# More pairs of the SwiGLU by block products, and a third tile for the second half of a pair's raw weights

## The chip, the cores and the metric

The kernel runs on one core of one Trainium2 chip. The metric is the time of one execution on the device in microseconds (us). A profile of one execution, with the start and the duration of every instruction, goes with it. The engines are TensorE (PE; its weight loads are listed apart as PEld), VectorE (DVE), ScalarE (ACT), GpSimd (POOL) and SyncE (SP), whose queue issues nearly all DMAs.

## The reference

One decoder layer over 512 tokens of width 1024 in float32: a SwiGLU FFN, a pair of gated token mixers (short convolution and Mamba-2), cross-attention over 256 memory tokens, a second SwiGLU FFN, and a final norm. The change touches the two FFNs alone.

```
def swiglu(u, w_gate_up, w_down):
    gate, up = jnp.split(u @ w_gate_up, 2, axis=-1)
    return (jax.nn.silu(gate) * up) @ w_down

h = h + 0.5 * swiglu(rmsnorm(h, ffn1_norm), ffn1_w_gate_up, ffn1_w_down)
...  mixers, attention
h = h + 0.5 * swiglu(rmsnorm(h, ffn2_norm), ffn2_w_gate_up, ffn2_w_down)
out = rmsnorm(h, final_norm)
```

The inner width is 2816, which is 22 groups of 128 columns. The kernel keeps float32 accuracy by splitting each operand into a rounded part `hi` and a remainder `lo` (type fp32r), and by three matmuls for each product: hi x hi, hi x lo, lo x hi.

## The kernel before

Activations lie transposed: a tile is 128 features by 512 tokens, and `u` is eight such tiles with their `hi` and `lo`. Weights come from HBM as raw float32 tiles of 128 x 1024, 512 KB each; ScalarE casts them to `hi` (L105), VectorE subtracts to get `lo` (L106), and PE loads them as stationary 128 x 128 blocks.

An FFN runs over 22 *pairs*, a pair being 128 columns of gate and the same 128 of up. Pairs go in blocks of 6, 8 and 8 (0 to 5, 6 to 13, 14 to 21). Behind each block stands the *down projection* of what the block made: eight jobs, whose results are added to `h` (L371, L373).

A pair is computed in one of two ways, chosen by `seven(ct)`:

- *Plain* (`plain`): two raw tiles in the ring `wr` (three tiles), split, and 48 matmuls of 512 tokens into two PSUM tiles.
- *By block products* (`seven_a`, `seven_b`): up and gate, the two halves of the feature axis and the two halves of the tokens make a product of 2 x 2 matrices of blocks. It is formed from seven block products instead of eight, each of 12 matmuls of 256 tokens, 84 in all. The sums of weight blocks are made on VectorE and then split: `sa` (L297, L298), the raw tile `ca` of the ring `wr` reused in place (L301), and `sb` (L304). Sums of tokens (`th`, `tl`) are made once for each FFN, behind pair 1 (`token_sums`).

`seven_a(n)` holds the first half of a pair: 24 matmuls with the split of `sa` (`wh`, `wl`), then 24 with the split of `ca` (`xh`, `xl`); each 24 are followed by a ScalarE copy out of PSUM and a VectorE add into `ev` (L309 to L314). `seven_b(n)` holds the second half: 12 matmuls with the split of `sb`, 24 with the split of the second raw tile `db`, and then L325, L326, L330, L331 and `act` (Silu, L270, the split of the result into `sh` and `sl`). `seven_b(n)` is emitted behind `seven_a(n+1)`, or behind the plain pair that follows.

A pair by block products has two PSUM tiles, A and B, from a pool of five for all users (`PJ`); the second 24 matmuls of pair n are written into the bank that B of pair n-2 held, which L326 reads last.

Raw tiles by block products: `ca` comes from the ring `wr` (L293), `db` from a tag of its own with two tiles (L294). Both are issued on the SP queue, in order, and each load waits until the tile that it overwrites has been read for the last time. For `db` that is the split `xl<-db`.

The order of instructions on each engine is set when the program is built, by a scheduler in the framework: it takes instructions from further down the text where it expects an engine to be free, and on the chip every engine then runs its list in that order.

Of the kernel before, what the change touches and what calls it, by code (L numbers as in the profile page):

```python
# [20 lines left out]
F32 = mybir.dt.float32  # L21
# [5 lines left out]
P = 128  # L27
# [18 lines left out]

def seven(ct):

    return ct >= 4 and ct % 3 != 0


COL = {}
# [10 lines left out]
def layer(ctx: ExitStack, tc: tile.TileContext, a, out):  # L63
# [13 lines left out]
    def nm(s):  # L77
        uid[0] += 1
        return f"{s}_{uid[0]}"

    def ps(tag="pj"):
        return psp.tile([P, T], F32, tag=tag, name=nm(tag), bufs=PJ if tag == "pj" else 8 - PJ)
# [21 lines left out]
    def split(src, hi, lo):  # L104
        S.copy(out=hi, in_=src)  # L105
        V.tensor_tensor(out=lo, in0=src, in1=hi, op=ALU.subtract)  # L106

    def ring(tag, dt=F32R):
        return wp.tile([P, 1024], dt, tag=tag, name=nm(tag), bufs=3)
# [93 lines left out]
    def ffn(gname, wgu, wd, fin=None):  # L203
        fs = ExitStack()
        fp = fs.enter_context(tc.tile_pool(name=nm("fp"), bufs=1, reuse_waits="tile"))
# [11 lines left out]
        def split_pair(src):  # L217

            ws = [fp.tile([P, 1280], F32R, tag=t, name=nm(t), bufs=2) for t in ("xh", "xl")]
            split(src.rearrange("p (a n) -> p a n", a=2),  # L220
                  *(t[:, :2 * (512 + OFF)].rearrange("p (a n) -> p a n", a=2)[:, :, :512]
                    for t in ws))
            return ws

        def mm3(pt, w, off, xs, start, stop):

            hi, lo = w
            for k in range(4):
                c = slice(off + k * P, off + (k + 1) * P)
                xh, xl = xs[k]  # L230
                TE.matmul(pt, hi[:, c], xh, start=start and k == 0, stop=False,  # L231
                          skip_group_check=True)
                TE.matmul(pt, hi[:, c], xl, start=False, stop=False, skip_group_check=True)  # L233
                TE.matmul(pt, lo[:, c], xh, start=False, stop=stop and k == 3,  # L234
                          skip_group_check=True)

        def quad(k0, i):
            c = slice(i * H, (i + 1) * H)
            return [(u[k0 + k][0][:, c], u[k0 + k][1][:, c]) for k in range(4)]

        def tsum(i):
            c = slice(i * H, (i + 1) * H)
            return [(x[0][:, c], x[1][:, c]) for x in tq]
# [45 lines left out]

        def seven_a(ct):  # L290
            ca = ring("wr", F32)
            db = fp.tile([P, 1024], F32, tag="db", name=nm("db"), bufs=2)
            nc.sync.dma_start(out=ca, in_=wgu[ct][:, :1024])  # L293
            nc.sync.dma_start(out=db, in_=wgu[ct][:, 1024:])  # L294
            c, a_, d, b = ca[:, :512], ca[:, 512:], db[:, :512], db[:, 512:]
            s31 = fp.tile([P, 1024], F32, tag="sa", name=nm("sa"), bufs=2)
            V.tensor_tensor(out=s31[:, 512:], in0=c, in1=d, op=ALU.add)  # L297
            V.tensor_tensor(out=s31[:, :512], in0=c, in1=a_, op=ALU.add)  # L298
            w31 = ring("wh"), ring("wl")
            split(s31, *w31)  # L300
            V.tensor_tensor(out=c, in0=a_, in1=s31[:, 512:], op=ALU.add)  # L301
            w2a = split_pair(ca)
            s4 = fp.tile([P, 512], F32, tag="sb", name=nm("sb"), bufs=2)
            V.tensor_tensor(out=s4, in0=c, in1=b, op=ALU.add)  # L304
            A, B = ps(), ps()
            mm3(B[:, 0:H], w31, 512, tsum(0), True, True)
            mm3(B[:, H:], w31, 0, tsum(1), False, True)
            ev = fp.tile([P, T], F32, tag="ev", name=nm("ev"), bufs=2)
            S.copy(out=ev[:, 0:H], in_=B[:, 0:H])  # L309
            V.tensor_tensor(out=ev[:, 0:H], in0=B[:, H:], in1=ev[:, 0:H], op=ALU.add)  # L310
            mm3(A[:, 0:H], w2a, 512 + OFF, quad(0, 0), True, True)
            mm3(A[:, H:], w2a, 0, tsum(2), False, True)
            S.copy(out=ev[:, H:], in_=A[:, H:])
            V.tensor_tensor(out=ev[:, H:], in0=A[:, 0:H], in1=ev[:, H:], op=ALU.add)  # L314
            return ct, A, B, ev, s4, db
# [18 lines left out]
        for b1 in range(KF % SB, KF + 1, SB):  # L334
            b0 = max(0, b1 - SB)
            wait = None
            for ct in range(b0, b1):
                if seven(ct):
                    nxt = seven_a(ct)
                    if wait is not None:  # L340
                        seven_b(*wait)
                    wait = nxt
                else:
                    p = plain(ct)
                    if ct == 0:
                        r = rms(h, D, wk)
                    plain_out(ct, *p)
                    if wait is not None:
                        seven_b(*wait)
                        wait = None  # L350
                if ct == 1:
                    token_sums()
# [50 lines left out]
    with tc.tile_pool(name="mx", bufs=1, reuse_waits="tile") as mx:  # L403
# [183 lines left out]
        for g in range(NG):  # L587
            bt, ct, xs = nxt
# [350 lines left out]
```

## Time and profile before

| | |
|---|---|
| median of 3 runs | 1577.1 us (1576.55 to 1578.83) |
| the profiled execution | 1577.46 us |
| its span, first to last instruction | 1575.7 us |
| PE busy | 1553.4 us (99%) |
| VectorE busy | 1035.4 us (66%) |
| ScalarE busy | 735.7 us (47%) |
| mean busy share of the DMA queues | q1, the SP queue's: 32.0% |

The profile page lists busy time by engine, the chain of work that ended last, and groups of instructions by source line with their count, mean duration and the idle time ahead of them. The timeline lists single instructions with start and duration in us; idle time ahead of one, and what ended it, stands in brackets. Tile names have their buffer numbers left out there. The first FFN runs from 6.4 us to 357.1, the second from 1213.7 to the end.

### The profile page before, as it was taken

How to read it: one execution, taken by the hardware profiler on the slowest of the kernel's cores; microseconds unless marked ns; L12 is line 12 of the kernel's file. 1: busy time of each engine (PE TensorE's matmuls, PEld its weight loads, DVE VectorE, ACT ScalarE, POOL GpSimd, SP SyncE). 2: the span in 40 equal slices, each digit the busy share in tenths (PEclk: the TensorE clock that was granted, in tenths of full speed). 3: DMA queues.
4: the chain of work that ended last, by engine and by line, in shares of the span. 5: the costliest groups of instructions: out<-in, count | busy, mean ns of one | idle time of the engine just before them, and what ended most of it. 6: DMA issues, size and time to landing. Idle time of an engine off the chain costs nothing.

```text
span 1575.7 us, 20708 instructions
## 1 busy us (share of the span) xinstructions
PE 1553.4 (99%) x8259; PEld 1315.2 (83%) x8259; DVE 1035.4 (66%) x1503; ACT 735.7 (47%) x1091; POOL 10.4 (1%) x22
## 2 busy tenths in 40 slices
PE   8999999999999999999999999999999999999998
PEld 6989989987878787787888888888888888988986
DVE  7767667667694777847564544665556867767754
ACT  8424324446787583935332222444344633433533
POOL 0000000011000000000000000000000000000000
PEclk9999999999999999999999999999999999999999
DMA  5333333235343424333243222235204233332321
GB/s 204 108 114 98 104 107 107 70 121 181 102 121 107 134 75 139 103 100 99 87 137 104 94 94 97 97 114 187 80 27 134 78 111 109 106 94 94 108 80 54
DMA packets 54065, 168.70 MB, mean 107 GB/s; under 512 B 6337, under 2 KB 6849, under 8 KB 53969
## 3 DMA queue, kind: packets, MB, share of 16 engines
q1 hardware_dynamic: 51952, 160.77, 32.0%
q0 software_dynamic: 1584, 5.31, 0.9%
q8 instruction: 64, 1.05, 0.3%
q10 hardware_dynamic: 432, 1.31, 0.2%
q14 instruction: 33, 0.26, 0.1%
HBM read 163.10 MB, written 4.26 MB: 106 GB/s over the span
## 4 chain that ended last, share of the span: by engine, by line
PE 94%; DVE 2%; DMA 2%; ACT 1%; issue 1%; ACTq 0%
PE pj L134 19%; PE pj L133 19%; PE pj L132 19%; PE pj L231 10%; PE pj L233 9%; PE pj L234 9%; DMA ea<-acd 1%; PE ss L557 1%; PE ss L508 1%; PE ss L562 1%; PE pj L692 0%; PE pj L691 0%; PE pj L693 0%; PE ss L496 0%; PE ss L160 0%
## 5 line engine op out<-in xcount | busy, mean ns | idle before, releaser
L105 ACT CAST wh<-wr 128x1024 fp32r<-128x1024 f32 (+2 forms) x251 | 243.8, 972 | 513.6 <-PE pj L133 370.3
L106 DVE TENSOR_TENSOR wl<-wr,wh 128x1024 fp32r<-128x1024 f32 (+2 forms) x251 | 281.6, 1125 | 93.5 <-ACT wh L105 93.3
L134 PE MATMUL pj<-uh,wl 128*128 128x512 f32 (+1 forms) x712 | 278.8, 393 | 3.5 <-DVE wl L106 3.5
L132 PE MATMUL pj<-uh,wh 128*128 128x512 f32 (+1 forms) x712 | 280.3, 394 | 0.0
L133 PE MATMUL pj<-ul,wh 128*128 128x512 f32 (+1 forms) x712 | 279.3, 392 | 0.0
L134 PEld LDWEIGHTS pj<-uh,wl 128*128 128x128 f32 (+1 forms) x712 | 133.5, 188 | 32.2 <-DVE wl L106 3.7
L231 PE MATMUL pj<-uh,wh 128*128 128x512 f32 (+1 forms) x416 | 152.9, 368 | 6.4 <-ACT uh L141 6.4
L132 PEld LDWEIGHTS pj<-uh,wh 128*128 128x128 f32 (+1 forms) x712 | 133.4, 187 | 28.2 <-issue 0.5
L133 PEld LDWEIGHTS pj<-ul,wh 128*128 128x128 f32 (+1 forms) x712 | 133.5, 188 | 28.0 <-issue 0.3
L233 PE MATMUL pj<-ul,wh 128*128 128x512 f32 (+1 forms) x416 | 152.6, 367 | 0.0
L234 PE MATMUL pj<-uh,wl 128*128 128x512 f32 (+1 forms) x416 | 151.9, 366 | 0.0
L133 PE MATMUL pj<-sl,wh 128*128 128x512 f32 x344 | 134.4, 391 | 0.2
L132 PE MATMUL pj<-sh,wh 128*128 128x512 f32 x344 | 134.1, 391 | 0.0
L134 PE MATMUL pj<-sh,wl 128*128 128x512 f32 x344 | 134.0, 389 | 0.0
L231 PEld LDWEIGHTS pj<-uh,wh 128*128 128x128 f32 x416 | 78.5, 189 | 20.1 <-ACT uh L141 6.6
L233 PEld LDWEIGHTS pj<-ul,wh 128*128 128x128 f32 x416 | 78.9, 190 | 13.2 <-DVE ul L142 0.7
L234 PEld LDWEIGHTS pj<-uh,wl 128*128 128x128 f32 x416 | 78.5, 189 | 12.5
L371 DVE SCALAR_TENSOR_TENSOR dn<-pj,r 128x512 f32<-128x512 f32 x47 | 32.5, 691 | 75.8 <-PE pj L134 75.7
L133 PEld LDWEIGHTS pj<-sl,wh 128*128 128x128 f32 x344 | 64.6, 188 | 14.8 <-DVE sl L106 1.9
L134 PEld LDWEIGHTS pj<-sh,wl 128*128 128x128 f32 x344 | 64.6, 188 | 13.3
L132 PEld LDWEIGHTS pj<-sh,wh 128*128 128x128 f32 x344 | 64.5, 188 | 13.3 <-ACT sh L105 0.2
L400 DVE SCALAR_TENSOR_TENSOR cv<-cx,prm,cv 128x510 f32<-128x510 f32 (+2 forms) x72 | 52.3, 744 | 5.4 <-ACT cv L397 5.2
(280 smaller groups left out, 3044.3 us busy)
## 6 DMA issues: line engine op xcount, KB each, us to landing
wr<-in_w_in SPq DMA_DIRECT2D x80, 512.0 KB, 3.2
wr<-in_w_gu SPq DMA_DIRECT2D x62, 512.0 KB, 3.8
wr<-in_w_d SPq DMA_DIRECT2D x32, 512.0 KB, 3.6
db<-in_w_gu SPq DMA_DIRECT2D x24, 512.0 KB, 3.9
m<-acd SPq DMA_DIRECT2D x32, 256.0 KB, 3.7
wr<-in_w_os SPq DMA_DIRECT2D x32, 256.0 KB, 3.1
wr<-in_w_d SPq DMA_DIRECT2D x16, 384.0 KB, 3.3
ea<-acd SPq DMA_DIRECT2D x32, 128.0 KB, 4.7
```

Of the source, the lines that this page charges most:

```text
L105: S.copy(out=hi, in_=src)
L106: V.tensor_tensor(out=lo, in0=src, in1=hi, op=ALU.subtract)
L132: TE.matmul(pt, hi[:, s_], xh, start=(k == 0), stop=False)
L133: TE.matmul(pt, hi[:, s_], xl, start=False, stop=False)
L134: TE.matmul(pt, lo[:, s_], xh, start=False, stop=(k == nk - 1))
L231: TE.matmul(pt, hi[:, c], xh, start=start and k == 0, stop=False, skip_group_check=True)
L233: TE.matmul(pt, hi[:, c], xl, start=False, stop=False, skip_group_check=True)
L234: TE.matmul(pt, lo[:, c], xh, start=False, stop=stop and k == 3, skip_group_check=True)
L371: V.scalar_tensor_tensor(out=dn, in0=pd, scalar=0.5, in1=r, op0=ALU.mult, op1=ALU.mult)
L400: V.scalar_tensor_tensor(out=acc[:, d:], in0=x[:, :T - d], scalar=pc(wname, j0 + j), in1=acc[:, d:], op0=ALU.mult, op1=ALU.add)
L508: TE.matmul(pst, btok[:, cs], xe, start=True, stop=True)
L557: TE.matmul(yd[64 * hh:64 * hh + 64, cs], xdt[c][:, q0:q0 + 64], ms[hh][:, cs], start=True, stop=True)
```

## The change

`seven(ct)` is true for every pair from the fourth on (ct >= 3) instead of for two of three from the fifth on, and the tag `db` has three tiles instead of two.

```
 def seven(ct):
-    return ct >= 4 and ct % 3 != 0
+    return ct >= 3
...
         def seven_a(ct):
             ca = ring("wr", F32)
-            db = fp.tile([P, 1024], F32, tag="db", name=nm("db"), bufs=2)
+            db = fp.tile([P, 1024], F32, tag="db", name=nm("db"), bufs=3)
             nc.sync.dma_start(out=ca, in_=wgu[ct][:, :1024])
             nc.sync.dma_start(out=db, in_=wgu[ct][:, 1024:])
```

In each FFN 19 pairs go by block products instead of 12: the pairs 3, 6, 9, 12, 15, 18 and 21 are new. Pair 3 stands in the block of six, the others in the blocks of eight, which now hold no plain pair at all.

Since the framework orders the instructions anew, three places are shown as they stand in the two programs (line, operation, out<-in, with the number of each tile).

VectorE in the first block of eight, from the split of one `db` tile to the L297 that reads the load which goes next into the same tag. Before (`db_1143` is pair 8, `db_1471` pair 11; pair 9 between them is plain):

```order
L106 TENSOR_TENSOR xl_1346<-db_1143,xh_1345 128x2x512
L326 TENSOR_TENSOR xx_1259<-pj_1088,ev_1113 128x512
L106 TENSOR_TENSOR wl_1342<-sb_1158,wh_1341 128x512
L330 TENSOR_TENSOR gt_1262<-pj_1087,r_245 128x256
L331 TENSOR_TENSOR gt_1262<-xx_1259,r_245 128x256
L304 TENSOR_TENSOR sb_1413<-wr_1397,db_1398 128x512
L106 TENSOR_TENSOR xl_1410<-wr_1397,xh_1409 128x2x512
L270 SCALAR_TENSOR_TENSOR gt_1262<-xx_1259,gt_1262 128x512
L297 TENSOR_TENSOR sa_1474<-wr_1470,db_1471 128x512
```

After (`db_1261` is pair 8, `db_1648` pair 11, which takes its tile; this row of nine comes again, with other numbers, in each pair of the block):

```order
L106 TENSOR_TENSOR xl_1467<-db_1261,xh_1466 128x2x512
L270 SCALAR_TENSOR_TENSOR gt_1380<-xx_1377,gt_1380 128x512
L301 TENSOR_TENSOR wr_1518<-wr_1518,sa_1522 128x512
L325 TENSOR_TENSOR xx_1506<-ev_1304 128x256
L304 TENSOR_TENSOR sb_1534<-wr_1518,db_1519 128x512
L106 TENSOR_TENSOR sl_1386<-gt_1380,sh_1385 128x512
L310 TENSOR_TENSOR ev_1433<-pj_1408,ev_1433 128x256
L106 TENSOR_TENSOR wl_1592<-sb_1405,wh_1591 128x512
L297 TENSOR_TENSOR sa_1651<-wr_1647,db_1648 128x512
```

Between the two rows stand seven instructions in both, of 512 columns or fewer after the change.

VectorE in the first block of the first FFN, at the end of the token sums (`tq`, `tl`). Before; `wl_411` is the second half of pair 2's weights, `wl_451` and `wl_481` are pair 3's, and `sa_521` belongs to pair 4:

```order
L255 SCALAR_TENSOR_TENSOR tq_368<-tq_368,ug_365 128x256
L106 TENSOR_TENSOR wl_411<-wr_409,wh_410 128x1024
L106 TENSOR_TENSOR sl_322<-gt_317,sh_321 128x512
L106 TENSOR_TENSOR tl_361<-tq_355,th_360 128x1024
L257 SCALAR_TENSOR_TENSOR tq_368<-tq_368,ug_365 128x256
L106 TENSOR_TENSOR wl_451<-wr_449,wh_450 128x1024
L106 TENSOR_TENSOR wl_481<-wr_479,wh_480 128x1024
L106 TENSOR_TENSOR tl_374<-tq_368,th_373 128x1024
L297 TENSOR_TENSOR sa_521<-wr_517,db_518 128x512
```

After; `sa_451` belongs to pair 3, `sa_524` to pair 4, and `wl_455` is the split of the first:

```order
L255 SCALAR_TENSOR_TENSOR tq_368<-tq_368,ug_365 128x256
L106 TENSOR_TENSOR sl_322<-gt_317,sh_321 128x512
L257 SCALAR_TENSOR_TENSOR tq_368<-tq_368,ug_365 128x256
L106 TENSOR_TENSOR tl_361<-tq_355,th_360 128x1024
L106 TENSOR_TENSOR wl_411<-wr_409,wh_410 128x1024
L106 TENSOR_TENSOR tl_374<-tq_368,th_373 128x1024
L297 TENSOR_TENSOR sa_451<-wr_447,db_448 128x512
L298 TENSOR_TENSOR sa_451<-wr_447 128x512
L297 TENSOR_TENSOR sa_524<-wr_520,db_521 128x512
L301 TENSOR_TENSOR wr_447<-wr_447,sa_451 128x512
L106 TENSOR_TENSOR wl_455<-sa_451,wh_454 128x1024
```

Pair 3's two plain splits are gone, pair 2's second split stands behind `sl_322`, L257 and `tl_361`, and the block products begin one pair earlier.

PE at the same place, the second half of pair 2 (`pj_377` and `pj_378` are its two PSUM tiles), as the difference of the two programs:

```order
 L231 MATMUL pj_377<-uh_138,wh_410 128x512
 L233 MATMUL pj_377<-ul_139,wh_410 128x512
+L231 MATMUL pj_378<-uh_138,wh_410 128x512
+L233 MATMUL pj_378<-ul_139,wh_410 128x512
 L234 MATMUL pj_377<-uh_138,wl_411 128x512
 L231 MATMUL pj_377<-uh_142,wh_410 128x512
```

Two matmuls that need only `wh_410` have moved ahead of the first one that needs `wl_411`.

More of the change, by code (lines that the diff above doesn't have):

```diff
@@ L47, in seven @@
 def seven(ct):
-    return ct >= 4 and ct % 3 != 0
+    return ct >= 3
 COL = {}
@@ L291, in seven_a @@
             ca = ring("wr", F32)
-            db = fp.tile([P, 1024], F32, tag="db", name=nm("db"), bufs=2)
+            db = fp.tile([P, 1024], F32, tag="db", name=nm("db"), bufs=3)
             nc.sync.dma_start(out=ca, in_=wgu[ct][:, :1024])
```

## The prediction

> **What bounds the kernel now.** I read the page's busy shares first, then the chain of waits, then windows over the FFN stages, then VectorE's timeline there.
>
> ```profile
> PE 1553.4 (99%) x8259; PEld 1315.2 (83%) x8259; DVE 1035.4 (66%) x1503; ACT 735.7 (47%) x1091; POOL 10.4 (1%) x22
> PE 94%; DVE 2%; DMA 2%; ACT 1%; issue 1%; ACTq 0%
> ```
>
> TensorE (PE) is 94% of the chain that ends last. The share alone proves little, since matmul ends are modelled; so here are four windows by stage (length, then busy time and instruction count of PE, its weight loads, VectorE (DVE) and ScalarE (ACT)): one plain pair (the third), two consecutive pairs by block products, and the two last blocks of eight pairs, one in each FFN.
>
> ```profile
> core 0: us, PE busy (x) PEld busy (x) DVE busy (x) ACT busy (x) POOL busy (x), PEclk, DMA share, GB/s
> 32.10:42.98 10.88, 10.88 (x49) 9.01 (x48) 10.88 (x18) 7.52 (x10) 0.00 (x0) 1.00 0.26 79
> 53.86:73.41 19.55, 19.55 (x170) 19.55 (x169) 14.15 (x23) 9.24 (x15) 0.00 (x0) 1.00 0.38 115
> 231.70:313.10 81.40, 81.40 (x565) 75.73 (x564) 56.58 (x83) 34.92 (x49) 0.00 (x0) 1.00 0.27 84
> 1436.40:1517.80 81.40, 81.40 (x565) 75.73 (x564) 56.68 (x83) 34.91 (x49) 0.00 (x0) 1.00 0.27 81
> ```
>
> The clock is 1.00 throughout. A plain pair takes 10.88 us for 48 matmuls, 227 ns each from start to start. Two block-product pairs take 19.55 us for 168 matmuls, so 9.78 us a pair and 116 ns each. A block of eight with five block-product pairs should then be 5 x 9.78 + 3 x 10.88 = 81.5 us: it is 81.40. So in these stages PE is fed without a gap, and VectorE, busy 56.6 us of the 81.4, waits for it.
>
> **The change part by part.** *PE.* Seven pairs in each FFN (3, 6, 9, 12, 15, 18, 21) go from 48 wide matmuls to 84 half as wide: 10.88 - 9.78 = 1.10 us saved each, 14 x 1.10 = **-15.5 us** as long as PE is fed.
>
> *VectorE.* What feeds PE grows. Its timeline inside a block gives the interval from one start to the next, where nothing is waited for:
>
> ```profile
> 133.93 0.68 DVE L106 TENSOR_TENSOR wl<-sb,wh 128x512 fp32r<-128x512 f32 x1
> 134.53 0.42 DVE L330 TENSOR_TENSOR gt<-pj,r 128x256 f32<-128x256 f32 x1
> 134.86 0.41 DVE L331 TENSOR_TENSOR gt<-xx,r 128x256 f32<-128x256 f32 x1
> 135.19 0.68 DVE L304 TENSOR_TENSOR sb<-wr,db 128x512 f32<-128x512 f32 x1
> 135.79 1.22 DVE L106 TENSOR_TENSOR xl<-wr,xh 128x1024 fp32r<-128x1024 f32 x1
> 136.93 0.68 DVE L270 SCALAR_TENSOR_TENSOR gt<-xx,gt 128x512 f32<-128x512 f32 x1
> ```
>
> So 0.60 us for 512 columns, 0.33 for 256, 1.14 for 1024 (less than the durations, which overlap). A plain pair costs VectorE two splits of 1024 and three passes of 512, 4.1 us. A block-product pair costs 16 instructions: three of 1024 (3.42), eight of 512 (L297, L298, L301, L304, the sb split, L326, L270, the sl split: 4.80) and five of 256 (L310, L314, L325, L330, L331: 1.67), together 9.9 us. Before, eight pairs are 5 x 9.9 + 3 x 4.1 = 61.8 us under 81.4 of PE. After, they are 79.2 us under 8 x 9.78 = 78.2 us: the cover is gone, and every wait of VectorE inside a block counts. ScalarE stays covered: four casts, Silu, the sh cast and two copies are under 6 us a pair.
>
> *Waits of VectorE.* L297 needs the `db` load, which may start only when the split of the old `db` has read it (the last row is of all 24 such loads):
>
> ```profile
> 124.08 1.23 DVE L106 TENSOR_TENSOR xl<-db,xh 128x1024 fp32r<-128x1024 f32 x1 [0.67 <-ACT xh L105]
> 130.04 0.69 DVE L297 TENSOR_TENSOR sa<-wr,db 128x512 f32<-128x512 f32 x1 [1.65 <-DMA db<-in_w_gu]
> 154.66 1.22 DVE L106 TENSOR_TENSOR xl<-db,xh 128x1024 fp32r<-128x1024 f32 x1
> 155.90 0.33 SPq L294 DMA_DIRECT2D db<-in_w_gu  x1
> 159.58 0.69 DVE L297 TENSOR_TENSOR sa<-wr,db 128x512 f32<-128x512 f32 x1 [0.82 <-DMA db<-in_w_gu]
> DMA to landing us min/median/max: 3.7/3.9/6.6
> ```
>
> The issue follows the end of the split by 0.02 us. From the split's start to L297 it took 4.92 us in one case and 5.96 in the other, where a `wr` load was in flight; with the median landing it is 1.22 + 0.02 + 3.9 = 5.14. With three tiles the split of pair n frees the tile for pair n+3, and the new order has seven instructions between that split and L297 of n+3: 1.14 + 5 x 0.60 + 2 x 0.33 = 4.8 us. So the third tile is just not enough: L297 waits 0.1 to 1.2 us in each period; I take 0.3, near the median and the 4.92 case, as the `wr` load is issued some 3.5 us before. The period of VectorE is then 9.9 + 0.3 = 10.2 us against 9.78: it loses 0.4 us a pair.
>
> The Trainium skill, page "DMA: Bandwidth & Descriptors", section "Anatomy of one DMA", gives a fit of 2.0 us plus bytes at 436 GB/s, made on the GpSimd path: an estimate of 3.2 us for these 512 KB. By it the wait vanishes and the sum below is about -12.6; this trace has 3.7 at the least, and I go by the trace.
>
> *Who waits for VectorE.* On PE the first to stall is the second group of a first half (the `xh`/`xl` of `ca`), which takes the PSUM bank that L326 of the pair two back has to read. Worked through by hand from the last down matmul as zero, with these intervals and ScalarE's cast:
>
> ```profile
> L105 ACT CAST xh<-db 128x1024 fp32r<-128x1024 f32 x24 | 25.2, 1050 | 27.5 <-issue 15.5 <-PE pj L233 12.1
> ```
>
> pair 6's `xl<-db` runs at 6.8 (PE done with the old `xh` at 5.6, cast 1.05), so pair 9's `db` lands at 11.9 while VectorE is ready at 10.1; L326 of pair 7 ends at 27.3, and PE asks for the bank at 27.8. From there VectorE loses 0.4 a pair: PE asks at 37.6, 47.4, 57.1 and gets at 37.5, 47.7, 57.0 (pair 13's half has no later L298 beside it). PE's lag is 0.4 us a block, and five waits stand in it, so each 0.1 us more in a wait adds 0.5. Bounds: 0 (VectorE keeps up) and 0.4 + 5 x 0.85 = 4.7 (every landing like the 5.96 case). I take **0.9** a block of eight, four blocks: **+3.6 us**. Behind the block the 8 down jobs take 43 us of PE and let VectorE catch up.
>
> *The first block of each FFN.* Pair 3 now needs the token sums 10.88 us earlier:
>
> ```profile
> 36.16 1.22 DVE L106 TENSOR_TENSOR wl<-wr,wh 128x1024 fp32r<-128x1024 f32 x1
> 37.54 0.39 PE L231 MATMUL pj<-uh,wh 128*128 128x512 f32 x1
> 39.37 2.36 DVE L106 TENSOR_TENSOR wl<-wr,wh 128x1024 fp32r<-128x1024 f32 x2
> 41.64 1.22 DVE L106 TENSOR_TENSOR tl<-tq,th 128x1024 fp32r<-128x1024 f32 x1
> 42.98 0.39 PE L231 MATMUL pj<-uh,wh 128*128 128x512 f32 x1
> 1245.96 1.22 DVE L106 TENSOR_TENSOR tl<-tq,th 128x1024 fp32r<-128x1024 f32 x1
> 1247.75 0.39 PE L231 MATMUL pj<-uh,wh 128*128 128x512 f32 x1
> ```
>
> Pair 3's two splits (39.37) go, but pair 2's second split (36.16) moves behind `sl`, the last L257 and a `tl`: from 36.2, 0.60 + 0.33, 0.1 for a cast, 1.14 + 1.14, it ends at 39.5. PE starts that half at 37.54 and, with the two matmuls moved ahead, needs it at 38.45: 1.0 us lost. Then the last `tl`, L297, L298, L297, L301 and the split of the sums end at 44.3, against PE at 44.0 and its third matmul at 44.2: 0.1. Behind it PE's group for pair 4 has a matmul on pair 4's `xh` ahead, which ScalarE casts late: 0.5. That is 1.6 us; in the second FFN, where the last `tl` starts 1.79 us ahead of pair 3 instead of 1.34 (1245.96 and 1247.75, 41.64 and 42.98), it is 1.2. Bounds 0 and 5; I take **+2.9** for both.
>
> *Sum:* -15.5 + 3.6 + 2.9 = -9.0 us. The profiled execution took 1577.46 us (span 1575.7, 1.8 around it), so 1568.5; the median of the runs is 0.4 lower: **1568**. Loads of weights into PE, the mixer and the attention keep their instructions.
>
> **The rivals.** *Full gain:* VectorE never late, as the 56.6 us of 81.4 suggest for a mean over a block; against it the 79.2 over 78.2. 1577.1 - 15.5 = 1561.6.
>
> *VectorE becomes the bound and the change is slower:* place L297 in every period of the blocks of eight, price 0.85 us a wait as in the 130.04 row: lag 4.7 a block, 18.8 in four, so -15.5 + 18.8 + 2.9 = +6.2, 1583. It decides once a wait costs 0.55 us more than I take in the base of 0.4, where the lag reaches (15.5 - 2.9)/4 = 3.1. For it: one of the two cases shown. Against: that case had two loads in flight, and the new order sets them 3.5 us apart.
>
> *Weight loads set PE's pace:* 84 loads a pair instead of 48. If a load's 188 ns were a matmul's interval, a pair would be 15.8 us and the kernel 14 x 4.9 slower, 1646:
>
> ```profile
> L231 PEld LDWEIGHTS pj<-th,wh 128*128 128x128 f32 x192 | 36.0, 188 | 0.2
> ```
>
> Against it the 116 ns of the second window, loads included; break-even is 48/84 of 227, 130 ns. The Trainium skill, "TensorE: Matmul & The Clock Gate", section "Back-to-back issue gap", gives sustained spacings of 81 ns at 128 columns and 131 at 512, by which 84 narrow matmuls (over 6.8 us) lose to 48 wide ones (6.3 us); by that rule this change is slower, and the trace's 116 and 227 disagree.
>
> **How the numbers follow.** Forecast (lag 0 to 2.5 a block): 65%, own range 1562.5 to 1574. Full gain: 15%. VectorE-bound: 13%, weight loads: 1%. Between forecast and slower lies a rest of 6% near no change. A measurement of this kernel tells about 0.2% (3.2 us) from no change. So faster 0.80, same 0.06, slower 0.14. The range 1561 to 1579 leaves out the worst of the VectorE-bound case and a little below the full gain.
>
> **What would show it.** Right: windows over the new blocks of eight of 78.2 to 80.5 us; VectorE busy there with about 79 us of starts, idle mostly at L297 on `db`, five times a block by some tenths; PE idle only ahead of a matmul with `xh` of `ca`, released by L326, and at pair 2's second split and pair 4's first group. Wrong: a block over 81.4 us, PE waiting at every period (VectorE-bound); blocks at 78.2 with no PE gap (full gain); spacing of the narrow matmuls over 118 ns; or ScalarE named as the releaser in the blocks, which I hold to be covered.

## The result and the profile after

The changed kernel took 1565.27 us (median of 4 runs, 1564.51 to 1566.80) against 1577.41 us for the kernel before beside it: a ratio of 0.9919, 95% interval 0.9906 to 0.9931, or -12.1 us. The forecast was 1568 us, 1561 to 1579, and "faster" with 0.80. The profiled execution took 1564.51 us, its span 1562.7. One of the twelve executions with the third tile alone took 2223.16 us at a granted clock of 0.655 and is left out of its median below.

The busy shares and the chain of waits on the page of the kernel after:

```profile
PE 1539.7 (99%) x8763; PEld 1327.3 (85%) x8763; DVE 1109.1 (71%) x1657; ACT 763.1 (49%) x1147; POOL 10.4 (1%) x22
PE 88%; DVE 5%; DMA 3%; ACT 2%; issue 1%; ACTq 0%
PE pj L134 20%; PE pj L132 20%; PE pj L133 20%; PE pj L231 7%; PE pj L234 7%; PE pj L233 7%; DMA db<-in_w_gu 2%; DVE xl L106 1%; PE ss L557 1%; DVE wl L106 1%; PE ss L508 1%; PE ss L562 1%; DMA ea<-acd 0%; PE pj L692 0%; PE pj L691 0%
```

VectorE (DVE) is 74 us busier, TensorE (PE) 14 us less, and the chain that ends last now leaves TensorE for 12% of the span instead of 6%: through the `db` load and the splits. The chain alone would suggest that much is lost there. The windows by stage say otherwise. The kernel after, first its two first blocks of six pairs, then its four blocks of eight (columns: length; busy time and count of each engine; granted clock; DMA share; GB/s):

```profile
core 0: us, PE busy (x) PEld busy (x) DVE busy (x) ACT busy (x) POOL busy (x), PEclk, DMA share, GB/s
6.60:74.50 67.90, 66.86 (x409) 59.38 (x410) 63.22 (x101) 47.16 (x69) 0.00 (x0) 1.00 0.49 164
1207.20:1271.80 64.60, 64.01 (x410) 57.64 (x409) 53.70 (x85) 38.18 (x53) 0.00 (x0) 1.00 0.36 112
```

```profile
107.50:185.90 78.40, 78.27 (x674) 78.09 (x673) 73.03 (x117) 40.87 (x61) 0.00 (x0) 1.00 0.36 115
229.40:307.80 78.40, 78.25 (x674) 78.06 (x673) 70.66 (x112) 41.12 (x61) 0.00 (x0) 1.00 0.28 88
1304.80:1383.30 78.50, 78.35 (x673) 78.12 (x672) 73.00 (x117) 40.80 (x61) 0.00 (x0) 1.00 0.36 115
1426.90:1505.30 78.40, 78.40 (x674) 78.10 (x673) 70.54 (x112) 40.95 (x61) 0.00 (x0) 1.00 0.28 88
```

The same two first blocks in the kernel before:

```profile
6.40:73.40 67.00, 67.00 (x372) 58.24 (x373) 57.82 (x89) 45.22 (x65) 0.00 (x0) 1.00 0.47 159
1213.70:1278.20 64.50, 64.50 (x374) 56.86 (x373) 48.48 (x74) 36.16 (x49) 0.00 (x0) 1.00 0.33 104
```

The second and fourth block of eight went from 81.4 us to 78.4. The difference of the spans, 13.0 us, is made up so: the blocks of eight with the down jobs behind them -3.4, -3.5, -3.2 and (without its down jobs) -3.0; the two first blocks with theirs +0.9 and +0.2; the start +0.2; the middle (mixers, attention; the same instructions) -0.7; the end -0.5. Some 0.3 us of the +0.9 have nothing to do with the change: the first matmuls of an execution are slow for a time that differs from execution to execution (last section). From its 41st matmul on, the first block of the first FFN takes 55.4 us before and 55.9 after.

**Where TensorE still waits.** In the first block of each FFN, at pair 2's second split and at pair 4's first group (timeline of the kernel after, VectorE's row first; beyond the spacing the gaps are 1.06 us at 40.07 and 0.61 at 1237.38, for pair 2, and 0.31 each at 51.13 and 1248.43, for pair 4, which are not shown):

```profile
38.79 1.22 DVE L106 TENSOR_TENSOR wl<-wr,wh 128x1024 fp32r<-128x1024 f32 x1
...
40.07 0.50 PE L234 MATMUL pj<-uh,wl 128*128 128x512 f32 x1 [0.90 <-DVE wl L106]
...
1237.38 0.50 PE L234 MATMUL pj<-uh,wl 128*128 128x512 f32 x1 [0.45 <-DVE wl L106]
```

In the blocks of eight, once or twice a block, ahead of the group on `xh` of `ca`. VectorE and then TensorE in the block that begins at 107.5:

```profile
150.46 0.69 DVE L297 TENSOR_TENSOR sa<-wr,db 128x512 f32<-128x512 f32 x1 [0.19 <-DMA db<-in_w_gu]
...
152.00 1.22 DVE L106 TENSOR_TENSOR xl<-wr,xh 128x1024 fp32r<-128x1024 f32 x1
153.14 1.22 DVE L106 TENSOR_TENSOR wl<-sa,wh 128x1024 fp32r<-128x1024 f32 x1
154.27 0.68 DVE L326 TENSOR_TENSOR xx<-pj,ev 128x512 f32<-128x512 f32 x1
```

```profile
154.70 0.28 PE L234 MATMUL pj<-th,wl 128*128 128x256 f32 x1
155.10 0.36 PE L231 MATMUL pj<-uh,xh 128*128 128x256 f32 x1
```

L326 ends at 154.95, and TensorE's matmul, due at 154.82, starts at 155.10. The profile's page lists 0.7 us of idle time ahead of these matmuls in the whole execution, and puts 0.2 of it down to VectorE's L326:

```profile
L231 PE MATMUL pj<-uh,xh 128*128 128x256 f32 x304 | 85.9, 282 | 0.7 <-DVE xx L326 0.2
```

**VectorE's own waits** in that block (waits view, in all, times, longest):

```profile
DVE sa L297 <- DMA db<-in_w_gu: 2.8, 3, 1.8
```

### The profile page after: what moved, and what is told of

The parts are those of the page before. It is cut to its first block, busy times and chain, and to the rows that moved or that the text cites. A ratio compares the mean times of both kernels' runs of the same rounds, so it can differ in the third digit from the quotient of the medians.

```text
span 1562.7 us, 21928 instructions
## 1 busy us (share of the span) xinstructions
PE 1539.7 (99%) x8763; PEld 1327.3 (85%) x8763; DVE 1109.1 (71%) x1657; ACT 763.1 (49%) x1147; POOL 10.4 (1%) x22
## 4 chain that ended last, share of the span: by engine, by line
PE 88%; DVE 5%; DMA 3%; ACT 2%; issue 1%; ACTq 0%
PE pj L134 20%; PE pj L132 20%; PE pj L133 20%; PE pj L231 7%; PE pj L234 7%; PE pj L233 7%; DMA db<-in_w_gu 2%; DVE xl L106 1%; PE ss L557 1%; DVE wl L106 1%; PE ss L508 1%; PE ss L562 1%; DMA ea<-acd 0%; PE pj L692 0%; PE pj L691 0%
## 5 line engine op out<-in xcount | busy, mean ns | idle before, releaser
L105 ACT CAST wh<-wr 128x1024 fp32r<-128x1024 f32 (+3 forms) x223 | 214.4, 963 | 448.5 <-PE pj L133 341.8
L106 DVE TENSOR_TENSOR wl<-wr,wh 128x1024 fp32r<-128x1024 f32 (+3 forms) x223 | 247.5, 1112 | 70.2 <-ACT wh L105 70.0
L134 PE MATMUL pj<-uh,wl 128*128 128x512 f32 (+1 forms) x712 | 279.3, 394 | 3.5 <-DVE wl L106 3.5
L132 PE MATMUL pj<-uh,wh 128*128 128x512 f32 (+1 forms) x712 | 280.7, 394 | 0.0
L133 PE MATMUL pj<-ul,wh 128*128 128x512 f32 (+1 forms) x712 | 279.6, 393 | 0.0
L231 PE MATMUL pj<-uh,xh 128*128 128x256 f32 x304 | 85.9, 282 | 0.7 <-DVE xx L326 0.2
L234 PE MATMUL pj<-uh,xl 128*128 128x256 f32 x304 | 85.4, 281 | 0.0
L233 PE MATMUL pj<-ul,xh 128*128 128x256 f32 x304 | 85.4, 281 | 0.0
L231 PE MATMUL pj<-th,xh 128*128 128x256 f32 x304 | 84.7, 279 | 0.0
L231 PE MATMUL pj<-th,wh 128*128 128x256 f32 x304 | 84.5, 278 | 0.0
```

Source lines behind the costliest of these rows:

```text
L132: TE.matmul(pt, hi[:, s_], xh, start=(k == 0), stop=False)
L133: TE.matmul(pt, hi[:, s_], xl, start=False, stop=False)
L134: TE.matmul(pt, lo[:, s_], xh, start=False, stop=(k == nk - 1))
```

## The experiments

Two theories stood against each other from the start. One, the prediction's: in the blocks of eight VectorE has no room left, so its period sets the pace, and each wait at L297 counts. The other: TensorE is the bound as before, and VectorE has room that the count over the block does not show.

### The third tile alone, and the pairs alone

The third tile alone is the kernel before with

```
-            db = fp.tile([P, 1024], F32, tag="db", name=nm("db"), bufs=2)
+            db = fp.tile([P, 1024], F32, tag="db", name=nm("db"), bufs=3)
```

> The third db tile alone; the pairs by block products are those of the kernel before (4, 5, 7, 8, ...). Theory (TensorE is the bound there and VectorE, 61.8 of 81.4 us busy in a block of eight, waits for it): no change, 1577 within 1 us, blocks of eight still 81.4 us. Rival (waits for the db load already cost time before): faster by some us.

Measured: 1576.77 us, ratio 0.9992 (0.9983 to 1.0001); the block at 232.6 takes 81.5 us. By itself the third tile is worth nothing.

The pairs alone, the kernel after with

```
-            db = fp.tile([P, 1024], F32, tag="db", name=nm("db"), bufs=3)
+            db = fp.tile([P, 1024], F32, tag="db", name=nm("db"), bufs=2)
```

> All pairs from the fourth on by block products, but two db tiles as before. Theory (VectorE is the bound in the blocks, and each of its waits counts): with two tiles the split of pair n frees the tile for pair n+2, and the order has some 2 us of work between that split and L297 of n+2, against about 5 us from the split's start to the landing; so L297 waits some 2.4 us a period (1.7 to 3), VectorE's period is about 12.4 us against 9.78 of TensorE, a block of eight takes 88 to 91 us, and the kernel 1600 to 1615. Rival (VectorE has room, the third tile is not needed): blocks of 78 to 79 us, 1565 to 1568.

Measured: 1642.85 us, ratio 1.0416 (1.0389 to 1.0442): 66 us slower than before, 78 slower than with the third tile. The sign is the first theory's, the size is past its band. Its four blocks take 98.3 to 100.1 us. The waits view of the first of them, VectorE's row and then TensorE's, and windows over a few us of it (TensorE's busy time, then the granted clock, DMA share, GB/s):

```profile
DVE sa L297 <- DMA db<-in_w_gu: 8.6, 4, 2.6
```

```profile
PE pj L231 <- ACT wh L105: 7.8, 5, 3.3
PE pj L234 <- DVE wl L106: 2.1, 4, 0.8
PE pj L231 <- ACT xh L105: 0.4, 1, 0.4
```

```profile
151.00:153.00 2.00, 2.00 (x13) 0.60 0.00 0
153.00:155.00 2.00, 2.00 (x12) 0.55 0.00 0
```

TensorE's named waits sum to 10.3 us in the block, the 10 to 13 us that were expected. Most of the other 10 us of 98.6 - 78.0 is the clock: in the block, 81 matmuls that stand some 0.21 us apart instead of 0.116 add up to about 8 us. The windows show one such stretch. Some 2 us behind a wait of 3.3 us, which ended at 149.43, the clock falls (0.60 and 0.55 are means over the windows; from 151.4 to 154.7 it is 0.50) and is back at 1.00 from 155. So here a wait of over 3 us costs about half as much again, behind it.

The Trainium skill, "TensorE: Matmul & The Clock Gate", section "HAM oscillation — how this bites in real kernels", gives as its rule that TensorE should have no idle gap over about 3.4 us, as its clock goes back to half behind one. The 3.3 us here lie just under that figure and brought the half clock all the same, and so did shorter waits in runs below; the measurement decides.

### Pair 3 by plain products again

The kernel after with

```
-    return ct >= 3
+    return ct >= 4
```

> The kernel after, but pair 3 of each FFN by plain products (twelve pairs changed instead of fourteen). Theory (the first block of each FFN gives back 2.8 us of its gain, measured as 1.06 + 0.31 us and 0.61 + 0.31 us of single gaps beyond the spacing plus smaller ones): these gaps go, two pairs cost 1.10 us more each, so -2.8 + 2.2 = -0.6 against the kernel after: 1564.7 (1564 to 1566). Rival (the gaps in the first block are there anyway): +2.2, 1567.5. Blocks of eight as in the kernel after, 78.4 us.

Measured: 1564.96 us, ratio 0.9919 (0.9907 to 0.9930), the same as the kernel after. The gaps of 1.06, 0.61 and 0.31 us in the first blocks went (windows of the run):

```profile
6.40:72.80 66.40, 66.40 (x372) 57.76 (x373) 57.77 (x90) 45.21 (x65) 0.00 (x0) 1.00 0.50 168
1206.10:1270.60 64.50, 64.50 (x374) 56.86 (x372) 48.48 (x74) 36.15 (x49) 0.00 (x0) 1.00 0.35 113
```

Busy time fills the 66.4 and 64.5 us, although each block holds 1.1 us more of matmuls than in the kernel after. The 66.4 are 1.5 us less than there, but 1.0 of that is a shorter opening of the execution; from the 41st matmul on it is 55.4 us against 55.9. The second FFN's block has 64.5 in both. The blocks of eight took 0.1 to 0.9 us more here, so the equal medians alone would not show it; by the blocks, two of the fourteen changed pairs, the two in the first blocks, gain nothing.

### A fourth tile

The first form takes the room from the tag `sa`, which the token sums share:

```
-            db = ... bufs=3)
+            db = ... bufs=4)
...
-            s31 = fp.tile([P, 1024], F32, tag="sa", name=nm("sa"), bufs=2)
+            s31 = fp.tile([P, 1024], F32, tag="sa", name=nm("sa"), bufs=1)
...
-                q = fp.tile([P, 1024], F32, tag="sa", name=nm("tq"), bufs=2)
+                q = fp.tile([P, 1024], F32, tag="sa", name=nm("tq"), bufs=1)
```

> The kernel after with four db tiles; the room for the fourth comes from the tag sa, which has one tile instead of two (VectorE writes each sa behind its own split of the one before). Theory (the waits at L297 are what makes VectorE late in the blocks): the split of pair n then frees the tile for n+4, a period earlier than needed; no wait on db in the blocks, no gap of TensorE in them: blocks 78.2 us instead of 78.4, -0.7 to -1.6 in four. The order of the first block changes with it: pair 2's second split stands twelve places earlier on VectorE, so TensorE's 1.06 and 0.61 us gaps should go, another -1.5 to -2.5. Together 1561 to 1563. Rival (the lag of the blocks is in VectorE's own work, 79.2 us in 78.2, and the load's landing is not what it waits for last): blocks stay 78.4.

Measured: 1574.77 us, ratio 0.9983 (0.9974 to 0.9991): 9.5 us slower than the kernel after. Half of the expectation came true, and half failed by the full sign (windows: one of the four blocks of eight between the two first blocks):

```profile
6.50:80.10 73.60, 68.40 (x408) 60.86 (x409) 63.95 (x100) 47.77 (x69) 0.00 (x0) 0.95 0.46 158
...
234.70:312.70 78.00, 78.00 (x674) 78.00 (x673) 71.69 (x114) 41.69 (x61) 0.00 (x0) 1.00 0.26 82
1212.30:1284.10 71.80, 66.55 (x409) 60.14 (x408) 54.85 (x85) 38.77 (x53) 0.00 (x0) 0.95 0.34 108
```

The blocks of eight have no gap left: 78.0 us, the 672 matmuls at 0.116. The first blocks take 5.7 and 7.2 us more. VectorE and TensorE there:

```profile
43.55 0.69 DVE L287 TENSOR_TENSOR gt<-pj,r 128x512 f32<-128x512 f32 x1 [0.81 <-PE pj L234]
...
45.29 0.68 DVE L268 TENSOR_TENSOR gt<-pj,gt 128x512 f32<-128x512 f32 x1
45.89 0.68 DVE L297 TENSOR_TENSOR sa<-wr,db 128x512 f32<-128x512 f32 x1
```

```profile
48.36 0.58 PE L231 MATMUL pj<-th,wh 128*128 128x256 f32 x1 [4.85 <-ACT wh L105]
```

The clock behind it, in a window of TensorE alone:

```profile
50.00:52.00 2.00, 2.00 (x11) 0.50 0.00 0
```

With one tile for the token sums the scheduler set the end of pair 2 (L287, L268) ahead of pair 3's sums (L297, L298). L287 reads pair 2's last matmul, so it cannot start before 43.5; the sums behind it, which need nothing of pair 2, start at 45.9, and TensorE has nothing to do for 4.85 us. The clock is 0.50 behind the gap, which makes the first blocks longer still.

To have the fourth tile without that order, the token sums were put into `db`'s tiles, which are empty at that time:

```
-                q = fp.tile([P, 1024], F32, tag="sa", name=nm("tq"), bufs=2)
+                q = fp.tile([P, 1024], F32, tag="db", name=nm("tq"), bufs=4)
```

with `db` at four tiles and `sa` at one as above.

> The kernel after with four db tiles again, but the room comes another way: tag sa has one tile, and the token sums are built in db's four tiles, which are empty then. On VectorE the order of the first block is close to that of the kernel after (pair 2's second split right behind the third tl, the L287 of pair 2 behind the sums of pair 3). Theory (the 10 us that the first four-tile kernel lost stand in the first block of each FFN alone, where L287 of pair 2, which waits for pair 2's last matmul, was set ahead of pair 3's sums on VectorE; the fourth tile itself takes the gaps out of the blocks of eight): blocks of eight 78.0 us, the first blocks as in the kernel after (67.9 and 64.5 us), together -1.6 against the kernel after, 1563.5 (1562.5 to 1565). Rival (one tile for sa is what costs, by its waits): first blocks of 70 us and more again, 1570 to 1575.

Measured: 1561.36 us, ratio 0.9904 (0.9889 to 0.9918). This kernel has four tiles for `db` and one for `sa` as the one before it, and the same number of instructions on each engine; the order of the first blocks differs, and 13.4 us go with it. So one tile for `sa` is not what cost; the order was. One of the blocks, the others alike:

```profile
106.50:184.50 78.00, 78.00 (x674) 78.00 (x673) 73.68 (x118) 41.62 (x61) 0.00 (x0) 1.00 0.36 116
```

and the first blocks take 67.1 and 64.2 us, with the 1.06 us gap still in the first. Two rows of VectorE in the block, and the first matmul of TensorE's group on `xh` of `ca`, which needs what L326 has read:

```profile
140.31 1.22 DVE L106 TENSOR_TENSOR wl<-sa,wh 128x1024 fp32r<-128x1024 f32 x1
141.44 0.68 DVE L326 TENSOR_TENSOR xx<-pj,ev 128x512 f32<-128x512 f32 x1
```

```profile
144.03 0.28 PE L231 MATMUL pj<-uh,xh 128*128 128x256 f32 x1
```

L326 stands behind the split `wl<-sa` here as it does in the kernel after, and ends 1.9 us before TensorE needs it; in the kernel after the same pair has 0.3 us left, and the next one none.

This kernel was then timed beside the unchanged kernel after on one chip:

> The kernel after, unchanged, beside the run that follows, so that the two are timed on one chip: 1565.3 (1564 to 1567).

> The kernel with four db tiles and the token sums in them, again, beside the kernel after: its profile had 1.6 us less in the blocks of eight, 1.1 us less in the two first blocks and 0.7 us less in the middle, which is the same code. If the gain is the first two, 2 to 3 us under the kernel after; if the 3.9 us between the medians of the two earlier sets were chance, 0 to 1 us.

Measured: 1564.54 us (ratio 0.9915, 0.9900 to 0.9931) and 1561.26 us (0.9901, 0.9887 to 0.9916). The difference is 3.3 us here and 3.9 between the sets, 0.2% and at the edge of what such sets can tell; the single times overlap (1561.3 to 1567.4 and 1560.7 to 1565.5). Where it comes from is seen in the profiles: no gap in the blocks, against 0.4 us a block in the kernel after, and no gap at pair 4 in the first blocks. In this second profile of the kernel after, with the same order of instructions, the gaps were 0.48, 0.00, 0.96 and 0.29 us in the four blocks, and VectorE's waits on `db` there 3.4, 2.5, 3.7 and 2.8 us in all: least where there is no gap, most where the gap is longest. So the size of the gap follows the landing of the loads, which differs from execution to execution.

With the fourth tile and pair 3 plain (`ct >= 4`) as well:

> As the run before, with pair 3 of each FFN by plain products, which gives the sums of the tokens a pair more of time. Theory: blocks of eight 78.0 us (0.5 to 1.4 less than in the pair-3-plain kernel with three tiles), first blocks 66.4 and 64.5 us as there: 1565.0 - 3.5 = 1561.5 (1560.5 to 1563.5), some 3 to 4 us under the kernel after, 0.2%. Rival (the gaps come back elsewhere): 1564 to 1566.

Measured: 1562.47 us (0.9914, 0.9899 to 0.9929), blocks of eight 78.0 us each, first blocks 67.0 and 64.5. Not told apart from the one with pair 3 by block products.

### More work for VectorE

L304 is done again in every pair by block products, without change to what is computed; here once more:

```
-            V.tensor_tensor(out=s4, in0=c, in1=b, op=ALU.add)
+            for _ in range(2): V.tensor_tensor(out=s4, in0=c, in1=b, op=ALU.add)
```

in the kernel after, and in the kernel before:

> The kernel after with L304 done twice in every pair by block products: 0.60 us more of VectorE a pair, the result the same. Theory (VectorE, 79.2 us of starts in 78.2 us, has no room left and its lateness adds up from pair to pair): its period is 10.5 to 10.8 us against 9.78, blocks of eight 80.5 to 84 us, TensorE waits ahead of xh of ca and of th on wh, the kernel 1574 to 1588. Rival (TensorE is the bound with room to spare): blocks within 0.5 us of 78.4, 1565 to 1567.

> The kernel before with L304 done twice in every pair by block products: the same 0.60 us a pair more, for the 24 pairs that it has. Theory: a block of eight holds 61.8 + 5 x 0.60 = 64.8 us of VectorE under 81.4 us of TensorE, so nothing changes: 1577 (1576 to 1579). If VectorE were already on the path: up to 24 x 0.60 = 14 us more.

Measured: 1569.32 us (0.9958, 0.9944 to 0.9972), +4.0 against the kernel after; and 1579.29 us (1.0011, 1.0002 to 1.0021), +2.3 against the kernel before, just above its band, with blocks of eight that stay at 81.5 us. The first of the two lies between the bands of both theories: +4.0 us is far from the 9 to 23 that the first named, and the rival's 1567 is exceeded as well, though its blocks are right. The profiled execution of the first has no gap in any block of eight, though VectorE has 4.8 us more to do in each; the gaps are 0.4 to 0.9 us in the down jobs (none to 0.3 in the kernel after), and the first blocks, that of the first FFN from its 41st matmul on, take 1.4 us more each. Down jobs and first blocks add 5.6 us and the blocks of eight give back 1.7, which makes the 4 us of the medians. (The profiled execution itself, 1564.87, was the shortest of its five: its opening and its middle, where nothing differs, were 3.7 us shorter than those of the kernel after.) The same piece of VectorE's list as above, in this run:

```profile
151.77 1.22 DVE L106 TENSOR_TENSOR xl<-wr,xh 128x1024 fp32r<-128x1024 f32 x1
152.90 0.69 DVE L297 TENSOR_TENSOR sa<-wr,db 128x512 f32<-128x512 f32 x1
153.50 0.69 DVE L326 TENSOR_TENSOR xx<-pj,ev 128x512 f32<-128x512 f32 x1
```

L326 stands ahead of the split `wl<-sa`, which a later pair needs, and not behind it: 1.4 us earlier, counted from the start of the block (108.2 here, 107.5 in the kernel after), with more work on the engine.

Twice and four times more:

> The kernel after with L304 done three times in every pair by block products: 1.20 us more of VectorE a pair. First theory (VectorE's period, now 11.1 us against 9.78, sets the pace): the lag grows by 1.3 us a pair, blocks of eight 82 to 86 us, the kernel 1585 to 1597. Second theory (VectorE works ahead in the down jobs before a block and catches up in those behind it, and what TensorE waits for is the place of L326 in VectorE's order, not VectorE's sum): with one repeat, blocks were 78.0 us and 0.4 to 0.9 us of gaps stood in the down jobs; with two, blocks of 78 to 80 us, up to 2 us in the down jobs, the kernel 1568 to 1578.

> The same with L304 done five times: 2.40 us more a pair, so 98 us of VectorE for the eight pairs in 78 us of TensorE, and with the 21 us of the eight down jobs about 120 in the 121.5 us of a block with its down jobs. Both theories have VectorE as the bound here, the second only by what is left when the lead and the down jobs are used up. First theory: lag 2.5 us a pair, 13 to 20 us a block, the kernel 1620 to 1650. Second: 5 to 12 us a block or in the down jobs behind it, the kernel 1590 to 1620.

Measured: 1576.93 us (0.9989, 0.9978 to 1.0000), +12.4 against the 1564.54 of the kernel after on the same chip, the upper end of the second theory's band; and 1632.03 us (1.0337, 1.0320 to 1.0354), the first theory's band. Windows of the blocks at 109 and 232.9 of the first, and at 113.4 and 251.5 of the second; then a stretch of the second, TensorE alone:

```profile
109.00:189.30 80.30, 79.20 (x673) 78.47 (x672) 80.10 (x130) 41.95 (x62) 0.00 (x0) 1.00 0.31 101
232.90:312.30 79.40, 78.94 (x673) 78.28 (x672) 76.80 (x124) 40.76 (x60) 0.00 (x0) 1.00 0.27 87
```

```profile
113.40:207.50 94.10, 85.13 (x673) 83.26 (x672) 89.98 (x145) 41.45 (x62) 0.00 (x0) 0.95 0.28 91
251.50:340.30 88.80, 82.80 (x674) 80.39 (x674) 86.13 (x140) 41.04 (x61) 0.00 (x0) 0.98 0.24 75
```

```profile
150.00:155.00 5.00, 3.51 (x16) 0.68 0.25 85
```

So with 4.8, 9.6 and 19.2 us more of VectorE in a block of eight, the blocks go from 78.4 to 78.0, 79.4 to 80.3, and 88.8 to 96.0. VectorE had some 8 us of room in a block, an estimate from the 9.6 us that cost 1 to 2. Past that each us of its work costs a us and more, since the clock then falls too (0.95; 0.68 in the 5 us around two waits of 1.7 and 1.0 us). The first blocks, of which only three pairs are by block products and which have no down jobs ahead of them, have much less room: with 1.8, 3.6 and 7.2 us more of VectorE they take 1.4, 2.3 to 3.9, and 5.8 us longer. Of the 12.4 us of two repeats about half stands there.

## Why the prediction was right, and where its steps were not

- **PE, -15.5 us.** Right in the blocks, somewhat small with what follows them. Once no gap is left, a block of eight takes 78.0 us (four-tile kernels), eight pairs of 9.75, and 81.4 - 78.0 is the 3.4 us of three pairs, where 3.3 were forecast. But a block with the down jobs behind it goes from some 125.3 to 121.5 us (122.4 to 118.5 for the last), 3.7 to 3.9: over four blocks about 2 us that the sum had at nothing. Part of it is a wait of 0.4 us in the down jobs behind the second and the fourth block of the kernel before, which is gone after; where the rest comes from isn't shown.
- **Blocks of 78.2 to 80.5 us, gaps only ahead of `xh` of `ca` behind L326, ScalarE no releaser there.** Right in place, releaser and size: 78.4 to 78.5 us.
- **The lag, 0.9 us a block.** Right in mechanism, mis-sized. The chain worked out by hand has L326 of pair 7 end 27.3 us into the block, and TensorE held up from 47.4 to 47.7; measured are 27.2, and 47.3 to 47.6 (the row at 155.10, less 107.51). It gave 0.3 to 0.4 us of lag, and the gaps measure 0.37 to 0.47; the 0.5 put on top for later landings was not there. Over four blocks that is 1.9 us. Between the spans the sum is off by 4.0 us (-9.0 against -13.0): these 1.9, the 2 us just named, and 0.7 in the middle, less what the start and the opening took the other way. So no errors of opposite sign hide behind the near hit: both mis-sized terms made the forecast too slow.
- **"The cover is gone, and every wait of VectorE inside a block counts."** This step failed, and with it the slope of 0.5 us a block for each 0.1 us in a wait, the 79 us of starts that the block was to hold, and the price of the VectorE-bound rival. It set 79.2 us of work against 78.2 us of block as if all of it had to lie inside the block. It does not. Where the eight L297 of one block stand, in the down jobs ahead of it and in the block (kernel after, windows of VectorE for line L297):

```profile
core 0: us, DVE busy (x), PEclk, DMA share, GB/s
185.90:229.40 43.50, 2.06 (x3) 1.00 0.32 97
229.40:307.80 78.40, 3.46 (x5) 1.00 0.28 88
```

  Three pairs' sums are made ahead, one for each `db` tile. By the timeline and the intervals of the prediction, 64.7 us of starts of pairs' work stand inside this block and 14.2 us in the 43.5 us of down jobs ahead of it, of which 2.5 are the tail of the block before. Inside the block VectorE's period is indeed longer than TensorE's 9.75: L326 comes every 10.0 us in the four-tile kernel and every 10.0 to 10.2 after the change. But it begins the block ahead, and that lead covers most of the loss. Counted over a block and its down jobs VectorE has room, and the repeats of L304 show how much.
- **VectorE waits 0.1 to 1.2 us at L297 in each period, taken as 0.3.** Right where its order holds. The row of nine that was said to come again in each pair comes in three of the five pairs whose L297 stands in a block: there the wait is 0.05 to 0.7 us, 0.28 in the mean of the twelve, and from the split's start to L297 it takes 4.9 to 5.5 us where 5.14 was worked out. In the first two pairs only four and six instructions stand between, and the waits are 1.7 to 1.9 and 0.7 to 1.2. In all that is 2.8 to 3.6 us a block by the waits view, twice the five times 0.3; the lag did not grow by it, since VectorE is early at the first of them: in the block at 107.5 L326 still ends 2.2 us before TensorE's group there, then 0.6, 0.3 and none.
- **What lets a wait reach TensorE.** Two things come together in the kernel after: the waits on `db`, and the place of L326 behind a split that nobody needs yet (1.1 us). Two runs show each without the other. With four tiles L326 stands behind that split in four pairs of every block, and no wait on `db` is left: it ends 1.8 us or more ahead of TensorE's group. With one repeat waits of 1.1 to 2.3 us a block are left, and from the third pair on L326 stands ahead of the split: it ends 0.6 us or more ahead. Neither run has a gap in a block.
- **The third tile is just not enough.** Right: the loads take 3.9 us at the median as before, L297 still waits for them, and with a fourth tile no wait on `db` is left. With the 3.2 us estimated from the Trainium skill, "DMA: Bandwidth & Descriptors", section "Anatomy of one DMA", the sum was -12.6, nearer to the -12.1 measured, but not for its reason: these loads took 3.6 us at the least.
- **First blocks, +2.9 us.** Right in place and size. Forecast were 1.0 and 0.5 us for the first FFN and 1.2 in all for the second; measured are 1.06 and 0.31, 0.61 and 0.31, plus 0.1 behind each. By the length of the blocks (55.4 to 55.9 from the 41st matmul on, and 64.5 in both) with the 1.1 us saved in each, 1.6 and 1.1 us were lost, where 1.6 and 1.2 had been worked out. With pair 3 plain both blocks are back at 55.4 and 64.5 us.
- **Rivals.** Full gain (1561.6): the kernel with four tiles and its 1561.3 is that case, or nearly. Weight loads as the pace: excluded, 84 loads a pair at 0.116 us a matmul in 78.0 us. VectorE-bound and slower (1583): its mechanism exists, but it wants some 10 us more of VectorE a block only to use up the gain (1576.93 us), or one tile less, not 0.55 us more in a wait. With two tiles it happened, at 1642.85.

## What to carry to other kernels

Busy time over a stage's length does not show whether an engine that feeds it has room: count its work over the stage and the stage ahead, in which it may already start, and ask how many buffers let it. A buffer count is part of the step that it serves; here one tile more was worth nothing alone and 78 us with the rest of the change. On engines that run in order, look at each change for an instruction that waits for something late (a read of the last matmul) ahead of work that nothing holds back: that cost 13 us between the two four-tile kernels, whose counts of instructions are equal.

## What was not expected of the hardware

- TensorE's clock falls behind its waits, and not only behind long ones. Behind 4.85 us without work it was granted 0.50 for 4.3 us, and for 6.2 us at the same place of the second FFN; behind 3.3 us, after some 2 us at full speed, 0.50 for 3.3 us; behind waits of 1.7 and 1.0 us that lay 1.3 us apart, 0.68 over 5 us. Behind the single 1.06 us of the kernel after it stayed at 1.00. The lengths alone don't decide it: with two repeats of L304 the same two waits, 1.6 and 0.6 us beyond the spacing, stand in both first blocks; behind those at 52.6 the clock was 1.00, behind those at 1256.2 it was 0.50 to 0.53 for 3.4 us. Some 8 of the 20.6 us that two tiles cost in a block came from the clock.
- The first matmuls of an execution stand 0.43 us apart instead of 0.23, until 9.8 to 12.7 us after the start of the span, while the column of the granted clock says 1.00. The first 40 took 11.0 to 12.3 us in the fourteen profiles, whatever the kernel. Why isn't shown; a first stage is compared behind its opening.
- The middle of the kernel, whose instructions are the same in all of them, took 853.1 to 859.2 us in these profiles (855.9 after, 856.6 before, 853.2 in the second profile of the kernel after). Differences of 3 us between two profiled executions are therefore read by stage, not by span.
